# Merge-gate projections as pairs of half-size products ahead of attention, and an attention loop one iteration deeper

## The chip, the core and the metric

The kernel runs on one core of a Trainium2 chip. The metric is the device time of one execution in microseconds, as the median of a few runs; lower is better. The engines are TensorE (PE, matrix products; PEld is its weight load), VectorE (DVE), ScalarE (ACT), GpSimd (POOL) and SyncE (SP, which only issues transfers). Each runs its own instructions in order and waits on semaphores for the others.

## What is computed

One layer of a hybrid trunk on 512 tokens with 1024 channels, all in float32. The parts that matter here:

```python
h = rms_norm(x, mix_norm_pre)
xa, ga, q, k, v, f, g_a, g_b = split(h @ w_in)
y_a = gelu(ga) * rg_lru(causal_dwconv(xa))             # recurrent branch, 1280 channels
y_b = forgetting_attention(q, k, v, f + b_forget)      # 16 heads of 64, per-frame causal
merged = (sigmoid(g_a + b_merge[0]) * (y_a @ w_proj_a)
          + sigmoid(g_b + b_merge[1]) * (y_b @ w_proj_b))
x = x + rms_norm(merged @ w_out, mix_norm_post)
# then: h @ w_up (1024 to 6144), a convolution over 3 tokens, gelu(gate) * value, @ w_down
```

`g_a` and `g_b` are the merge gates: two products of `h` with 1024 x 1024 weights. The sigmoid is computed as a tanh of half the argument; the missing "+1" and "x 0.5" come where the gate is used.

## The kernel before

**Exactness.** PE multiplies in a rounded format, so every float32 operand is split into a high part (a cast on ACT, in lines 172, 696, 756 and others) and a low part (operand minus high part, on DVE, line 175 and others); a product is three matmuls: high x high, high x low, low x high (`mm3`, lines 222 to 224).

**Weights.** `order` lists the weight units in the order in which they are used. `fetch` (through `Split`) loads a unit on SP's queue, casts it and subtracts; `unit(name, ahead)` first fetches up to `ahead` units further. The pool `weights` has four buffers each for raw, high and low tiles, shared by all units.

**Tiles.** A projection tile (`project`) is 128 output channels by 512 tokens: 8 blocks of input channels x 3 matmuls of width 512 into one PSUM bank, of which there are eight.

**Stages.** The recurrent branch's projections (xa, v, ga), then pa, which is `y_a @ w_proj_a` in eight tiles of two units each (order `PA_ORDER`), with transfers for a later stage issued in the background (`background`) and the forget gates (`forget`) within it. Then the attention loop over eight pairs of heads, p = 0 to 7: the q and k tiles; the halves of both; the transposes of the previous pair's probabilities (`pt`); the gate tile ma p, whose tanh multiplies `pa[:, p]` on DVE (line 793); the product with the values for the previous pair (`av`); the scores of this pair (`scores`). `prep_alloc` fills the two bias tiles B (one for each head of a pair; two buffers) on POOL's queue: a broadcast copy from DRAM (line 686), then two adds of the mask by DMA (line 689). `scores` reduces each block of scores with its bias on DVE (line 719), which also frees the bank and, after the last block, the bias tile; the exponentials follow on ACT, and `normalise` scales the rows on DVE. Behind the loop come the mb gate tiles, alternating with pb, which is `y_b @ w_proj_b`, and the merge.

**Pairs.** The up-projection already uses a seven-product scheme (Strassen's, in Winograd's form): two tiles of 128 channels, each 8 blocks by 512 tokens, are seen as 2 x 2 blocks and computed by seven products of half the input channels and half the tokens, 12 matmuls of width 256 each, in place of two tiles of 24 matmuls of width 512. A `Pair` holds two raw weight tiles, splits the plain quarters (`plain_low`, `plain_high`; the low part by a negated cast on ACT and an adding DMA on POOL's queue), forms sums of weight quarters (`sums`, split by `sums_hi` and `sums_lo`) and multiplies with token sums `sh`, `sl`. `keep` copies a partial result that is added to another later. `period` writes out by hand one pair's course, interleaved with the pair before it and the two after it.

**What sets the order.** Most instructions are ordered on each engine by a planner that simulates the program with estimated costs and takes, of what it thinks ready, what was written first. Under `tc.manual_schedule()` (around the up pairs, for example) the written order is kept on every engine. `reuse_waits="tile"` and `bufs` say how many buffers a tile name has: a new tile waits until the last reader of the buffer's former tile has finished, and a pool opened where another was closed waits for the tiles that lay there.

Of the kernel before, what the change touches and what calls it, by code (L numbers as in the profile page):

```python
# [63 lines left out]
def kernel(  # L64
# [124 lines left out]
    order += [(f"pa{e}_{i}", w_pa[2 * e + i], (5, P)) for e, i in PA_ORDER]  # L189
    for p in range(KD):  # L190
        order.append((f"q{p}", *cols(w_in, B_Q + p)))
        order.append((f"k{p}", *cols(w_in, B_K + p)))
        order.append((f"ma{p}", *cols(w_in, B_MA + p)))
    order += [(f"mb{e}", *cols(w_in, B_MB + e)) for e in range(3)]
    for e in range(KD):
        if e >= 3:
            order.append((f"mb{e}", *cols(w_in, B_MB + e)))
        order.append((f"pb{e}", *cols(w_pb, e)))
# [110 lines left out]
    def v_out(c, pv):  # L309
        for t in range(NT):  # L310
            pvv = pv[t].rearrange("p (q j d) -> p q j d", q=4, j=2)
            for q in range(4):
                p = 4 * c + q
                vh = vt[p][:, t, 0:4:3, :]
                act.copy(vh, pvv[:, q])
                dve.tensor_tensor(out=vt[p][:, t, 1:3, :], in0=pvv[:, q], in1=vh.bitcast(F32), op=ALU.subtract)

    with ExitStack() as rg:
# [235 lines left out]
        vpools.append(mstk.enter_context(tc.tile_pool(name="vy1", bufs=5, reuse_waits="tile")))  # L554
        tpool = rg.enter_context(tc.tile_pool(name="rtanh", bufs=TR, side="right", reuse_waits="tile"))
        gpool = rg.enter_context(tc.tile_pool(name="gelu", bufs=2, side="right", reuse_waits="tile"))
# [90 lines left out]

        pps = {}
        for e, half in PA_ORDER:
            if half == 0:  # L650
                pps[e] = bank(f"pa{e}")
            wh, wl = unit(f"pa{e}_{half}")
# [6 lines left out]
            if (e, half) == (4, 1):  # L659
                forget()  # L660

    tgpool = mstk.enter_context(tc.tile_pool(name="tg", bufs=3, reuse_waits="tile"))

    def gate_tile(e, which):
        c = 0 if which == "ma" else KD
        pg = bank(f"{which}{e}")
        project(pg, unit(f"{which}{e}"), hh, hl)
        tg = tgpool.tile([P, S], F32, tag="tg", name=f"tg_{which}{e}")
        act.activation(out=tg, in_=pg, func=AF.Tanh, scale=0.5, bias=hb[:, c + e : c + e + 1])
        return tg  # L670

    with ExitStack() as at:
# [20 lines left out]
        def halves(ps, name):  # L693
            hi = apool.tile([P, S], F32R, tag=f"{name[0]}h", name=f"h_{name}")
            lo = apool.tile([P, S], F32R, tag=f"{name[0]}l", name=f"l_{name}")
            act.copy(hi, ps)
            dve.tensor_tensor(out=lo, in0=ps, in1=hi.bitcast(F32), op=ALU.subtract)
            return hi, lo

        def scores(p, q, k, bias):  # L700
# [11 lines left out]
            for j in range(2):  # L712
                h = 2 * p + j
                Pt = apool.tile([P, PO[NT]], F32, tag="P", name=f"P{h}")
# [46 lines left out]
        def av(p, pts):  # L761
            y = apool.tile([P, S], F32, tag="y", name=f"y{p}", bufs=2)
            tmp = apool.tile([P, S], F32, tag="ytmp", name=f"ytmp{p}", bufs=2)
# [12 lines left out]
            yb[p] = vpools[p == 0 or p > 4].tile([P, 2, S], F32R, tag="vy", name=f"yb{p}")  # L776
            act.copy(yb[p][:, 0], y)
            dve.tensor_tensor(out=yb[p][:, 1], in0=y, in1=yb[p][:, 0].bitcast(F32), op=ALU.subtract)

        prev = None  # L780
        for p in range(KD):
            bias = prep_alloc(p)
            pq, pk = bank(f"q{p}"), bank(f"k{p}")
            project(pq, unit(f"q{p}"), hh, hl)
            if prev is not None:
                normalise(prev)
            project(pk, unit(f"k{p}"), hh, hl)
            q = halves(pq, f"q{p}")
            k = halves(pk, f"k{p}")
            if prev is not None:  # L790
                pts = pt(p - 1, prev)
            tg = gate_tile(p, "ma")
            dve.scalar_tensor_tensor(out=pa[:, p], in0=tg, scalar=1.0, in1=pa[:, p], op0=ALU.add, op1=ALU.mult)
# [17 lines left out]
    ml = mgpool.tile([P, KD, S], F32R, name="ml")  # L811
    for e in range(KD):
        if e >= 3:
            tgs.append(gate_tile(e, "mb"))
        pb = bank(f"pb{e}")
        wh, wl = unit(f"pb{e}")
        for k in range(KD):
            mm3(pb, wh[:, k], wl[:, k], yb[k][:, 0], yb[k][:, 1], k == 0, k == KD - 1)
        tg = tgs[e]
        dve.scalar_tensor_tensor(out=tg, in0=tg, scalar=1.0, in1=pb, op0=ALU.add, op1=ALU.mult)  # L820
# [21 lines left out]
    KH, SH = KD // 2, S // 2  # L842

    def sub(out, a, b):
        dve.tensor_tensor(out=out, in0=a, in1=b, op=ALU.subtract)  # L845

    A, B = slice(0, 512), slice(512, 1024)
    X, Y = slice(0, SH), slice(SH, S)

    def quarter(a, b, s):  # L850
        return tuple(x[:, s].rearrange("p (k e) -> p k e", k=KH) for x in (a, b))

    class Pair:


        def __init__(self, j):
            self.j = j
            self.r = [wpool.tile([P, D], F32, tag="raw", name=f"raw_up{e}") for e in (j, j + JF)]
            for r, e in zip(self.r, (j, j + JF)):
                nc.sync.dma_start(r, w_up[e])  # L860
            self.w, self.t, self.th, self.x, self.ml = {}, {}, {}, {}, {}

        def plain_low(self, i):

            src = self.plain_src(i)
            l = self.ml[i] = stpools[i].tile([P, (D, 512)[i]], F32R, tag=f"ml{i}", name=f"ml{i}_{self.j}")
            act.activation(out=l, in_=src, func=AF.Copy, scale=-1.0)  # L867
            nc.gpsimd.dma_start(l, src, accum_op=ALU.add)  # L868

        def plain_src(self, i):  # L870
            return (self.r[0], self.r[1][:, B])[i]

        def plain_high(self, i):
            src = self.plain_src(i)
            h = stpools[i].tile([P, (D, 512)[i]], F32R, tag=f"mh{i}", name=f"mh{i}_{self.j}")
            act.copy(h, src)
            l = self.ml.get(i)
            if l is None:
                l = stpools[i].tile([P, (D, 512)[i]], F32R, tag=f"ml{i}", name=f"ml{i}_{self.j}")
                sub(l, src, h.bitcast(F32))  # L880
            if i == 0:
                self.w[1], self.w[2] = quarter(h, l, A), quarter(h, l, B)
            else:
                self.w[3] = quarter(h, l, A)

        def plain(self, i):
            self.plain_low(i)
            self.plain_high(i)

        def sums(self, i):  # L890
            r0, r1 = self.r
            t = self.t[i] = tpool.tile([P, D], F32, tag="t", name=f"t{i}_{self.j}")
            if i == 0:
                sub(t[:, A], r1[:, A], r0[:, A])
                sub(t[:, B], r1[:, B], r1[:, A])
            else:
                sub(t[:, A], r1[:, B], self.t[0][:, A])
                sub(t[:, B], r0[:, B], t[:, A])

# [191 lines left out]
    def period(j, n1, n2, load):  # L1091
# [33 lines left out]
        if b:  # L1125
            gelu(b.g)
# [375 lines left out]
```

## Time and profile before

| | us |
|---|---|
| median of 3 runs | 927.29 (927.29 to 927.44) |
| span of the profiled execution, first to last instruction | 924.2 |
| median less that span (the profiled execution's own total isn't printed) | 3.1 |
| granted PE clock over the span | 0.997 |
| pa stage, first matmul of pa to first of q | 190.8 to 248.9 |
| attention loop to the first mb tile | 248.9 to 426.2 |
| mb and pb to the first wo tile | 426.2 to 517.6 |

A profile line of a group reads: line of the kernel, engine, operation, tile written <- tiles read, shape, count, then busy time and mean ns, then the idle time of the engine before it and what ended that. In a timeline line the two first numbers are the start and the length in us. A line number can be that of a helper that many tiles share.

### The profile page before, as it was taken

The page shows a single profiled execution, that of the slowest core. Times are in us where ns is not written, and L with a number is a line of the kernel's source. Part 1 is how long each engine was busy: PE and PEld are TensorE (multiplying, and loading weights), DVE is VectorE, ACT ScalarE, POOL GpSimd, SP SyncE. Part 2 cuts the span into 40 slices and gives each one's busy share as a digit, 9 for nine tenths or more (in the row PEclk, how much of TensorE's full clock was granted, in tenths as well). Part 3 has the DMA queues.
Part 4 walks back from the last instruction along what each step waited for, and adds up shares of the span by engine and source line. Part 5 has one row for each costly group of instructions (what it writes and reads, how often), then busy time and mean ns, then how long its engine had stood idle before and what let it go on. Part 6 is the DMA issues. An engine that isn't in the chain of part 4 may idle for free.

```text
span 924.2 us, 14992 instructions
## 1 busy us (share of the span) xinstructions
PE 911.7 (99%) x5582; PEld 796.1 (86%) x5582; DVE 685.2 (74%) x1121; ACT 568.8 (62%) x982; POOL 230.6 (25%) x240
## 2 busy tenths in 40 slices
PE   8999999999999999999999999999999999999996
PEld 7988888887888888888888889999999999978885
DVE  5866369632857777777644588999999999889897
ACT  7555495433345566666423376688888888676664
POOL 4134345444242232220111000042323323100001
PEclk9999999999999999999999999999999999999998
DMA  7677589989776566553232755188898888799764
GB/s 278 216 227 208 165 207 256 270 211 253 176 229 152 160 148 157 151 150 86 69 114 91 271 182 163 34 212 235 218 238 204 234 208 211 223 372 325 240 201 142
DMA packets 76282, 182.29 MB, mean 197 GB/s; under 512 B 7281, under 2 KB 35745, under 8 KB 75826
## 3 DMA queue, kind: packets, MB, share of 16 engines
q1 hardware_dynamic: 45056, 123.13, 39.5%
q0 software_dynamic: 30864, 57.68, 30.2%
q8 instruction: 44, 0.72, 0.3%
q10 hardware_dynamic: 290, 0.53, 0.1%
q14 instruction: 28, 0.23, 0.1%
HBM read 148.59 MB, written 33.64 MB: 197 GB/s over the span
## 4 chain that ended last, share of the span: by engine, by line
PE 94%; DVE 2%; DMA 1%; issue 1%; ACT 0%; POOL 0%; SPq 0%; DVEq 0%; POOLq 0%
PE up L924 7%; PE up L922 7%; PE up L921 7%; PE dn L1225 4%; PE dn L1224 4%; PE dn L1223 4%; PE pa L223 2%; PE ga L224 2%; PE ga L223 2%; PE pa L224 2%; PE pa L222 2%; PE ga L222 2%; PE q L222 2%; PE ma L222 2%; PE wo L838 2%; PE mb L222 2%
## 5 line engine op out<-in xcount | busy, mean ns | idle before, releaser
L868 POOL DMA_DIRECT2D ml<-raw_up x41 | 35.0, 855 | 154.8 <-ACT ml L867 79.2
L1076 DVE SCALAR_TENSOR_TENSOR u<-up,cpt,u 128x511 f32<-128x511 f32 x96 | 71.2, 745 | 2.6 <-ACT u L1070 0.9
L1225 PE MATMUL dn<-wh_dn,al 128*128 128x512 f32 x168 | 65.6, 391 | 0.9 <-DVE al L845 0.8
L1224 PE MATMUL dn<-wl_dn,ah 128*128 128x512 f32 x168 | 65.4, 389 | 0.0
L1223 PE MATMUL dn<-wh_dn,ah 128*128 128x512 f32 x168 | 65.4, 389 | 0.0
L921 PE MATMUL up<-sh,th 128*128 128x256 f32 x252 | 60.4, 277 | 0.5 <-ACT x L928 0.5
L922 PE MATMUL up<-sl,th 128*128 128x256 f32 x252 | 60.2, 276 | 0.0
L175 DVE TENSOR_TENSOR wl_dn<-raw_dn,wh_dn 128x1024 fp32r<-128x1024 f32 x42 | 51.5, 1226 | 9.1 <-ACT wh_dn L172 9.1
L172 ACT CAST wh_dn<-raw_dn 128x1024 fp32r<-128x1024 f32 x42 | 44.1, 1050 | 17.5 <-issue 10.3
L845 DVE TENSOR_TENSOR tl<-t,th 128x1024 fp32r<-128x1024 f32 x42 | 51.1, 1218 | 1.3 <-ACT th L902 1.3
L1084 POOL TENSOR_TENSOR yf<-u,u 128x512 f32<-128x512 f32 x24 | 32.0, 1333 | 71.8 <-issue 47.5
L1070 ACT ACTIVATE u<-up,cpt 128x512 f32<-128x512 f32 x48 | 36.9, 778 | 19.8 <-PE up L924 11.0
L921 PEld LDWEIGHTS up<-sh,th 128*128 128x128 f32 x252 | 47.3, 188 | 0.7 <-ACT x L928 0.7
L922 PEld LDWEIGHTS up<-sl,th 128*128 128x128 f32 x252 | 47.3, 188 | 0.0
L902 ACT CAST th<-t 128x1024 fp32r<-128x1024 f32 x42 | 43.9, 1045 | 4.5 <-DVE t L845 1.8
L689 POOL DMA_DIRECT2D B<-maskf x32 | 39.1, 1628 | 27.2 <-DMA B<-cnd 24.1
L922 PE MATMUL up<-h2l,mh 128*128 128x256 f32 x168 | 40.2, 276 | 0.0
L921 PE MATMUL up<-h2h,mh 128*128 128x256 f32 x168 | 40.2, 276 | 0.0
L924 PE MATMUL up<-sh,tl 128*128 128x256 f32 x252 | 38.8, 276 | 0.0
L1225 PEld LDWEIGHTS dn<-wh_dn,al 128*128 128x128 f32 x168 | 31.5, 188 | 8.1 <-DVE al L845 1.7
L175 DVE TENSOR_TENSOR wl_pa<-raw_pa,wh_pa 128x640 fp32r<-128x640 f32 x16 | 13.1, 819 | 32.8 <-ACT wh_pa L172 32.8
L1224 PEld LDWEIGHTS dn<-wl_dn,ah 128*128 128x128 f32 x168 | 31.5, 188 | 6.6
(654 smaller groups left out, 3167.7 us busy)
## 6 DMA issues: line engine op xcount, KB each, us to landing
raw_up<-in_w_up_dram SPq DMA_DIRECT2D x48, 512.0 KB, 5.4
td<-in_w_down_dram POOLq DMA_DIRECT2D x36, 512.0 KB, 5.9
raw_dn<-td SPq DMA_DIRECT2D x24, 512.0 KB, 5.0
B<-cnd POOLq DMA_DIRECT2D x16, 640.0 KB, 4.8
ml<-raw_up POOLq DMA_DIRECT2D x20, 512.0 KB, 5.3
raw_dn<-in_w_down_dram SPq DMA_DIRECT2D x18, 512.0 KB, 3.5
raw_wo<-in_w_out_dram SPq DMA_DIRECT2D x16, 512.0 KB, 3.8
td<-td POOLq DMA_DIRECT2D x12, 512.0 KB, 10.8
```

The lines of the kernel that those rows point to most:

```text
L172: act.copy(self.wh, self.raw)
L175: engine.tensor_tensor(out=self.wl, in0=self.raw, in1=self.wh.bitcast(F32), op=ALU.subtract)
L222: pe.matmul(dst, ah, bh, start=first, stop=False)
L845: dve.tensor_tensor(out=out, in0=a, in1=b, op=ALU.subtract)
L902: act.copy(self.th[i], self.t[i])
L921: pe.matmul(dst, wh[:, k], ah[:, k], start=first and k == 0, stop=False, skip_group_check=True)
L922: pe.matmul(dst, wh[:, k], al[:, k], start=False, stop=False, skip_group_check=True)
L924: pe.matmul(dst, wl[:, k], ah[:, k], start=False, stop=k == KH - 1, skip_group_check=True)
L1076: dve.scalar_tensor_tensor(out=c[:, s:], in0=ps[:, : S - s], scalar=col(C_CFW + 3 * e + j), in1=c[:, s:], op0=ALU.mult, op1=ALU.add)
L1223: pe.matmul(dst[t], ah[:, k, tok], wh[:, k], start=first, stop=False, skip_group_check=True)
L1224: pe.matmul(dst[t], ah[:, k, tok], wl[:, k], start=False, stop=False, skip_group_check=True)
L1225: pe.matmul(dst[t], al[:, k, tok], wh[:, k], start=False, stop=last, skip_group_check=True)
```

## The change

- Fourteen of the sixteen merge-gate tiles (ma 0 to 7, mb 0 to 5) become seven pairs of the seven-product scheme, in a stage of their own between pa and attention. `Pair` and `period` move up and take their source block, token sums, pools and epilogue as parameters (`Halved`). The up-projection uses the same classes as before.
- The token sums of `h` and the first gate pair's weight sums are formed within the pa stage (`early_sums`, called after each of its 16 steps); `forget` moves from the step (4, 1), the tenth, to the fourth.
- The tile mb6 is computed alone between pa and the first pair; the tile mb7 alone in the last attention iteration.
- An ma gate multiplies `pa` at once; an mb gate is written to DRAM (`gmb`) and read back while pb runs.
- After the last pair come q0 and k0, whose weights are fetched within the hand-written order.
- The attention loop has no gate tile. In iteration p: scores of p, the q tile of p + 1, transposes of p - 1, the k tile of p + 1 and both halves, av of p - 1, normalise of p. The probabilities get four buffers in place of two; the halves of q and k and one small tile get one in place of two.
- Parts of pb 0, 1 and 2 are computed at the end of attention; the rest behind it.

The core of the diff:

```diff
+            elif step == 12:
+                gp[0] = Pair(gates, 0, GP[0])
+            elif step == 13:
+                gp[0].sums(0)
+                gp[0].sums(1)
...
-            wh, wl = unit(f"pa{e}_{half}")
+            wh, wl = unit(f"pa{e}_{half}", min(2, len(PA_ORDER) - step))
...
+    def gate_use(name, tg):
+        e = int(name[2])
+        if name[:2] == "ma":
+            dve.scalar_tensor_tensor(out=pa[:, e], in0=tg, scalar=1.0, in1=pa[:, e], op0=ALU.add, op1=ALU.mult)
+        else:
+            nc.sync.dma_start(gmb[e], tg)
...
+    gate_tile("mb6", 0)
+    with ExitStack() as g2:
...
+        gp[1] = Pair(gates, 1, GP[1])
+        man = g2.enter_context(ExitStack())
+        man.enter_context(tc.manual_schedule())
+        for i, f in enumerate((fq[3], fq[0], fq[2], fq[1])):
+            act.copy(gates.sh[i], f)
+            sub(gates.sl[i], f, gates.sh[i].bitcast(F32))
...
+        p.plain_high(0)
+        p.plain_high(1)
+        p.p5()
+        p.p12()
+        n.sums(0)
+        n.sums(1)
+        n.plain_low(0)
+        p.keep(2, p.a[:, Y])
+        p.add(p.a[:, X], p.a[:, X], 2)
+        p.keep(1, p.c[:, X])
...
+        def more(j):
+            if j + 3 < len(GP):
+                gp[j + 3] = Pair(gates, j + 3, GP[j + 3])
+            elif j + 2 < len(GP):
+                pass
+            else:
+                fetch(where[("q0", "k0")[j + 2 - len(GP)]])
+
+        for j in range(len(GP)):
+            period(gp[j], gp.get(j - 1), gp.get(j + 1, none), gp.get(j + 2, none), gate_epilogue, lambda: more(j))
+            gp.pop(j - 1, None)
+        b = gp.pop(len(GP) - 1)
+        b.add(b.c[:, Y], b.a[:, Y], 1)
+        b.add(b.c[:, X], b.c[:, X], 0)
+        gate_epilogue(b, "c", 0)
+        pq = bank("q0")
+        project(pq, unit("q0", 0), hh, hl)
+        gate_epilogue(b, "c", 1)
+        pk = bank("k0")
+        project(pk, unit("k0", 0), hh, hl)
+        b.product(4, b.a[:, Y])
...
         for p in range(KD):
-            bias = prep_alloc(p)
-            pq, pk = bank(f"q{p}"), bank(f"k{p}")
-            project(pq, unit(f"q{p}"), hh, hl)
-            if prev is not None:
-                normalise(prev)
-            project(pk, unit(f"k{p}"), hh, hl)
-            q = halves(pq, f"q{p}")
-            k = halves(pk, f"k{p}")
+            now = scores(p, q, k, bias)
+            if p < KD - 1:
+                bias = prep_alloc(p + 1)
+                pq = bank(f"q{p + 1}")
+                project(pq, unit(f"q{p + 1}"), hh, hl)
+            else:
+                gate_tile("mb7", 2)
             if prev is not None:
                 pts = pt(p - 1, prev)
-            tg = gate_tile(p, "ma")
-            dve.scalar_tensor_tensor(out=pa[:, p], in0=tg, scalar=1.0, in1=pa[:, p], op0=ALU.add, op1=ALU.mult)
+            if p < KD - 1:
+                pk = bank(f"k{p + 1}")
+                project(pk, unit(f"k{p + 1}"), hh, hl)
+                q, k = halves(pq, f"q{p + 1}"), halves(pk, f"k{p + 1}")
+            else:
+                pb_part(0, range(KD - 2))
             if prev is not None:
                 av(p - 1, pts)
-            prev = scores(p, q, k, bias)
-        tgs = [gate_tile(0, "mb")]
-        normalise(prev)
-        tgs.append(gate_tile(1, "mb"))
+            normalise(now)
+            prev = now
         pts = pt(KD - 1, prev)
-        tgs.append(gate_tile(2, "mb"))
+        pb_part(1, range(KD - 1))
         av(KD - 1, pts)
+        pb_part(0, range(KD - 2, KD - 1))
+        pb_part(2, range(KD - 1))
```

More of the change, by code (lines that the diff above doesn't have):

```diff
@@ L189 @@
     order += [(f"pa{e}_{i}", w_pa[2 * e + i], (5, P)) for e, i in PA_ORDER]
+    order.append(("mb6", *cols(w_in, B_MB + 6)))
     for p in range(KD):
@@ L192 @@
         order.append((f"k{p}", *cols(w_in, B_K + p)))
[L193 to L198, printed above, removed]
+    order.append(("mb7", *cols(w_in, B_MB + 7)))
+    order += [(f"pb{e}", *cols(w_pb, e)) for e in range(KD)]
     for ph in range(2):
@@ L658 @@
                 act.copy(pa[:, e], pps[e])
[L659 to L669, printed above, removed]
-        return tg
+            early_sums(step)
@@ L672 @@
+    dstk.close()
     with ExitStack() as at:
```

405 lines of the change are left out of this document (254 added, 151 removed).

## The prediction

> **What bounds the kernel now.** I read the page, then the waits of TensorE (PE), the matmuls of single tiles, the chain of waits, the table of stages, and last the timelines of one attention iteration.
>
> ```profile
> span 924.2 us, 14992 instructions
> PE 911.7 (99%) x5582; PEld 796.1 (86%) x5582; DVE 685.2 (74%) x1121; ACT 568.8 (62%) x982; POOL 230.6 (25%) x240
> PE 94%; DVE 2%; DMA 1%; issue 1%; ACT 0%; POOL 0%; SPq 0%; DVEq 0%; POOLq 0%
> ```
>
> PE is busy for 99% of the span and carries 94% of the chain that ended last. The waits of PE (line, releaser, us in total, times, longest) hold only a few us; two of them matter here:
>
> ```profile
> PE up L924 <- DMA ml<-raw_up: 0.9, 1, 0.9
> ...
> PE up L921 <- ACT x L928: 0.5, 1, 0.5
> ```
>
> So the time falls by what PE no longer executes, unless a new wait appears. These two, 1.4 us together, stand where the up-projection begins its half-size products; the change builds a second such beginning.
>
> How long is a tile, and how long a pair? Busy times overlap (matmuls are pipelined), so I take distances between starts. The ga tiles' row gives first and last start (us) of the first matmul of each group of three; the chain gives the same place of the pair loop ten pairs apart.
>
> ```profile
> L222 PE MATMUL ga<-hh,wh_ga x80: 389/389/390, 136.4 to 190.1; 128*128 128x512 f32 x80
> ```
> ```profile
> 621.33 0.45 PE up L924 x4
> ...
> 716.93 0.45 PE up L924 x4
> ```
> ```profile
> 621.33:716.93 95.60, 95.60 (x842) 95.60 (x842) 89.45 (x133) 79.62 (x121) 30.28 (x31) 1.00 0.89 224
> 190.80:249.00 58.20, 58.20 (x258) 47.10 (x257) 27.96 (x35) 19.80 (x29) 23.63 (x27) 1.00 0.97 214
> 301.25:323.94 22.69, 22.69 (x154) 19.06 (x156) 16.65 (x43) 13.82 (x34) 4.95 (x7) 1.00 0.58 156
> 437.40:517.60 80.20, 80.20 (x394) 66.84 (x394) 39.11 (x39) 27.56 (x40) 8.98 (x7) 1.00 0.32 102
> ```
>
> From 136.4 to 190.1 lie 79 groups of three matmuls: 0.2266 us each, 5.44 us for a tile of 24. Ten pairs of seven products run in 95.60 us: 9.56 us a pair of 84 half-width matmuls, 0.114 us each, 1.37 us a product. In the table (length; busy PE, weight load, DVE, ACT, POOL; clock; DMA share; GB/s) PE is full in all four stages and the clock is 1.00.
>
> **The change, term by term.**
>
> *The products.* A gate pair has the same 84 matmuls, of the same shapes and alternation, as an up pair. Fourteen tiles cost 14 x 5.44 = 76.2 us, seven pairs 7 x 9.56 = 66.9: **9.2 us less** PE work. In that stage the other engines do less than in the up stage, where DVE was busy 89.45 of 95.60 with the convolution taps and PE waited for nothing; the gate stage has two tanh and at most two DVE products a pair instead of four taps. So the steady gate periods are put at 9.56 with no wait. The Trainium skill, "TensorE: Matmul & The Clock Gate" (Back-to-back issue gap), speaks for a smaller gain: it gives N/2.4 + 2.5 ns, a fixed part for each matmul that seven half-size products pay 84 times and two tiles 48 times; by that a pair would save an estimated 1.2 us, the seven 8.3. The trace has 0.114 against 0.227, a ratio of one half with no fixed part left to see, and it decides.
>
> *Work put before the gates.* Beside the pa products DVE gets eight 1024-wide adds or subtractions for the token sums, four 512-wide ones for the first pair and two 1024-wide splits; ACT two casts. Their lengths, and those of what leaves the attention loop (four iterations, mean ns after the bar):
>
> ```profile
> L175 DVE TENSOR_TENSOR wl_ma<-raw_ma,wh_ma 128x1024 fp32r<-128x1024 f32 x4 | 4.9, 1224 | 13.9 <-ACT wh_ma L172 13.9
> L793 DVE SCALAR_TENSOR_TENSOR pa<-tg_ma,pa 128x512 f32<-128x512 f32 x4 | 2.7, 684 | 0.0
> ```
> ```profile
> L172 ACT CAST wh_ma<-raw_ma 128x1024 fp32r<-128x1024 f32 x5 | 5.2, 1047 | 19.5 <-issue 19.5
> L669 ACT ACTIVATE tg_ma<-ma,hb 128x512 f32<-128x512 f32 x4 | 2.7, 680 | 0.0
> ```
>
> 10 x 1.22 + 4 x 0.68 = 14.9 us of DVE go into a stage with 30 us free: nothing, unless one blocks a weight split in DVE's order. The first pair's 1 MB comes over DMA engines that are 97% busy there; its raw tiles are needed some 10 us later, and I count nothing.
>
> *The beginning of the gate stage.* PE's cover is the mb6 tile, 5.44, and p5, 1.37. Meanwhile ACT casts four token sums (4.2 us) and DVE subtracts them (4.9), then splits the plain quarter. If they start with mb6, they fit. If ACT's order puts the tanh of mb6 first, p5 waits 0.68 + 1.05 + 1.22 = 2.95, and the low part of product 1, due at 2.95 + 1.37 + 0.91 = 5.23, waits for five DVE subtractions, 0.68 + 1.05 + 6.1 = 7.8: 5.5 in all. Between 0 and 5.5 I take the 1.4 that the other such beginning shows: **+1.4**.
>
> *q0 and k0 fetched in the hand-written order.* Their cast and split stand in ACT's and DVE's order ahead of the sums of the next pair. The cast of q0 needs one of four buffers, and two pairs hold all four until product 7. Then 1.05 + 1.22, and two adds of this kind:
>
> ```profile
> 638.62 0.43 DVE L940 TENSOR_TENSOR up<-up,x 128x256 f32<-128x256 f32 x1
> ```
>
> together 3.1, against two products, 2.73, that PE has meanwhile: **+0.4**, from 0 to 2 if the load lands late behind the gate writes on SP's queue. Behind k0's split stand only adds that 10.9 us of q0 and k0 cover.
>
> *Attention.* One iteration of PE before (start, us):
>
> ```profile
> 301.18 0.71 PE L746 MATMUL pt<-ident,P 64*128 64x64 f32 x16
> ...
> 302.56 0.50 PE L222 MATMUL ma<-hh,wh_ma 128*128 128x512 f32 x1
> ...
> 308.14 0.39 PE L770 MATMUL av<-PTh,v 128*128 128x512 f32 x1
> ...
> 310.71 0.49 PE L710 MATMUL s4c<-h_k,h_q 64*128 64x512 f32 x1
> ...
> 312.78 0.50 PE L222 MATMUL q<-hh,wh_q 128*128 128x512 f32 x1
> ...
> 318.34 0.39 PE L222 MATMUL k<-hh,wh_k 128*128 128x512 f32 x1
> ```
>
> Transposes 1.4, ma 5.6, av 2.6, scores 2.1, q 5.6, k 5.5. Without ma the loop is 22.7 - 5.6 = 17.1 us. DVE keeps 16.65 - 1.22 - 0.68 = 14.75 of it, ACT 12.1: busier, not the bound. Two covers shrink. First, k's halves: before, the transposes and ma lay between k and av; now only av does.
>
> ```profile
> 303.32 0.68 DVE L697 TENSOR_TENSOR l_k<-k,h_k 128x512 fp32r<-128x512 f32 x1
> ...
> 306.71 0.47 DVE L757 TENSOR_TENSOR PTl<-pt_r,PTh 128x128 fp32r<-128x128 f32 x2
> ```
>
> l_k ended at 304.0, 2.8 us after k (301.18), with a weight split just ahead of it; the second matmul of scores needs it 2.6 + 0.3 after k. That is even: **+0.7** (0.1 in each of seven), from 0 to 3.5. Second, the bias tiles B. There are two, for the even and the odd head, refilled only after the reductions of scores have read them, by a copy and two masked adds each, in order on POOL's queue:
>
> ```profile
> 312.99 0.68 DVE L719 CUSTOM_DVE_ANT_0 P<-s5c,B 128x512 f32<-128x512 f32 x1
> ...
> 316.27 0.08 DVE L719 DVE_READ_ACCUMULATOR2_ANT mx<- 128x1 f32 x1
> ```
> ```profile
> 315.96 1.25 POOL L686 DMA_DIRECT2D B<-cnd  x2 [13.42 <-DVE mx L719]
> 320.98 2.46 POOL L689 DMA_DIRECT2D B<-maskf  x2 [3.76 <-DMA B<-cnd]
> 323.89 2.40 POOL L689 DMA_DIRECT2D B<-maskf  x2 [0.45 <-DMA B<-cnd]
> ```
> ```profile
> DMA to landing us min/median/max: 3.0/5.5/7.6
> ```
>
> (The last line is that of all masked adds.) The odd tile is first read at 313.0 and free at 316.35; its last add is issued at 325.1 and lands at a median 5.5 later, 330.6. The loop of this buffer is 17.6 us: hidden in 22.7, even with 17.1. The transposes need the score banks 2.1 + 5.6 = 7.7 after scores begin, the reductions end 5.6 after (316.35): 2 us of slack. The first iteration has neither transposes nor av, so the second scores follow after 2.1 + 5.6 + 5.5 = 13.2, 4.4 before the odd tile: 4.4 - 2 = **+2.4**, once. It is 0 if DVE takes the reductions in another order, 6 if the first B must also wait for gate tiles in the same memory, which are read until q0.
>
> *The end.* The transposes' copies took from 301.18 to 307.2, 6.0; in the last iteration 18 matmuls of pb0 (4.1) and the transposes (1.4) cover them: **+0.5**, 0 to 1.5. The mb gates go through DRAM, 2 MB out and 2 MB back, the latter in a stage with a DMA share of 0.32: nothing.
>
> **Sum:** -9.2 + 1.4 + 0.4 + 0.7 + 2.4 + 0.5 = **-3.8 us** on a span of 924.2. The runs' median, 927.29, has 3.1 us around the span, which nothing here touches: **923.5**. By the bounds it is from -9.2 (918.1) to +9.3 (936.6).
>
> **Rivals.** *Every cover holds* (-6.5 to -9.2, about 919): for it, the up stage has run this sequence without a wait and the loop's engines have 14% or more left; against it, three margins are even. Chance 0.22. *The bias loop becomes the bound, and the kernel gets slower*: one landing at 7.6 in place of 5.5 makes the loop 19.7, 2.6 more than PE's 17.1, and what is late stays late: seven iterations lose 18, less 2 of slack, 16, in place of the 2.4 above, +10 in all (937). It decides from a loop of 18.5, where 7 x 1.4 - 2 = 7.8 with the other 3.0 eats the 9.2 and more. For it: refills closer together raise the DMA share; against it: landings at the median. With 1.6 a loop over PE's in place of 2.6 it is 930. Chance 0.19. *The gain comes and is given back* at several of these places, within 0.2%: 0.12. The rest, 0.47, is the forecast, -1.9 to -6.5; in it lies that half-size products keep a fixed cost which the up stage doesn't show (the 0.9 less gain of the page's rule, 924.4), a chance of 0.02 after the ratio above.
>
> Faster by over 0.2% (1.9 us, about what a measurement here can tell from no change) is 0.47 + 0.22 = 0.69; slower 0.19. The range, 918.6 to 930.0, leaves out the very best and the upper half of the slow case.
>
> **What would show it.** Right: seven gate periods of 9.56, an attention loop of 17.1 to 17.6, and PE waits of 3 to 8 us in all, for the gate sums at the start, for DVE's reductions at the first transposes, and for l_k. The bias rival: POOL's adds landing after scores in every iteration, a loop over 18.5. Wrong altogether: gate periods over 9.56, or waits in pa for weight splits behind the token sums.

## The result: slower by 0.9%, and the profile after

| | before | after |
|---|---|---|
| median, us (range, runs) | 927.37 (927.29 to 928.62, 4) | 936.65 (934.84 to 937.35, 4) |
| span of the profiled execution | 924.2 | 935.6 |
| end of pa to first wo matmul | 248.9 to 517.6 | 249.0 to 526.8 |

The ratio of the times is 1.0091, 95% interval 1.0076 to 1.0105; by the medians the change costs 9.3 us, where 3.8 less were forecast. The profiled execution of the kernel after is the slowest of its four, 937.35 us. The page of the kernel after says so in three lines: its span, TensorE's busy time, and the shares of the chain that ended last.

```profile
span 935.6 us, 15714 instructions
PE 911.4 (97%) x5834; PEld 803.7 (86%) x5834; DVE 724.7 (77%) x1184; ACT 596.9 (64%) x1033; POOL 243.1 (26%) x252
PE 84%; DMA 7%; DVE 3%; issue 3%; POOL 1%; ACT 1%; SPq 0%; DVEq 0%; POOLq 0%; ACTq 0%
```

PE carried 94% of the chain before and carries 84% now; transfers have 7%. The table of stages finds the place (length; busy PE, weight load, DVE, ACT, POOL; clock; DMA share; GB/s). The stages are the gate pairs, q0 to product 4, attention's opening from S(0) to the end of S(2), one steady iteration, and mb7's start to the first wo. S(p), PT(p), av(p) are scores, transposes and the product with the values of iteration p.

```profile
254.44:326.06 71.62, 68.12 (x578) 67.31 (x576) 46.93 (x68) 47.35 (x73) 11.42 (x15) 1.00 0.67 176
326.06:338.56 12.50, 12.49 (x64) 10.41 (x62) 5.37 (x7) 5.80 (x8) 3.05 (x3) 1.00 0.93 296
338.56:382.33 43.77, 36.95 (x225) 28.76 (x225) 26.95 (x74) 20.76 (x53) 14.53 (x14) 0.92 0.74 190
382.33:399.73 17.40, 17.40 (x131) 14.58 (x129) 14.84 (x42) 12.18 (x32) 6.02 (x6) 1.00 0.68 168
469.31:526.79 57.48, 57.47 (x330) 48.04 (x329) 39.01 (x71) 26.49 (x56) 13.39 (x7) 1.00 0.43 148
```

Two stages have holes: the gate pairs (3.5 us) and the opening of attention (6.8 us of 43.77, and the only clock below 1.00). The steady iteration is full. PE's waits between 245 and 385 us name them:

```profile
PE s2c L981 <- ACT h_k L967: 4.5, 1, 4.5
PE ma L409 <- DMA gml<-raw_ma: 1.7, 1, 1.7
PE ma L406 <- DVE ma L425: 1.3, 1, 1.3
PE s4c L981 <- DVE l_k L968: 1.0, 1, 1.0
PE s0c L981 <- DVE l_k L968: 0.6, 1, 0.6
```

S(1) waits 4.5 us for h_k, a cast of 0.58 us. Why is it late? The chain of waits, PE's pieces left out (start, length):

```profile
324.71 3.70 DMA raw_k<-in_w_in_dram
...
328.43 1.06 ACT wh_k L172
...
329.51 0.22 DVE wl_k L175
...
330.65 0.44 DVE mb L425
...
331.64 0.57 POOL B L957
...
332.49 0.75 POOL B L960
333.25 13.31 DMA B<-maskf
...
352.13 4.13 DMA B<-cnd
...
359.60 7.60 DMA B<-maskf
```

POOL's timeline shows the link in the middle, ACT's the last one:

```profile
316.99 0.55 POOL L957 DMA_DIRECT2D B<-cnd  x1 [2.68 <-DVE gtl L318]
...
331.64 0.57 POOL L957 DMA_DIRECT2D B<-cnd  x1 [13.78 <-DVE mb L425]
332.49 2.48 POOL L960 DMA_DIRECT2D B<-maskf  x2 [0.28 <-issue]
341.62 2.39 POOL L960 DMA_DIRECT2D B<-maskf  x2 [6.66 <-DMA B<-cnd]
```
```profile
347.47 0.72 ACT L995 ACTIVATE P<-P,mx 128x512 f32<-128x512 f32 x1 [7.43 <-DVE mx L990]
...
350.49 0.72 ACT L995 ACTIVATE P<-P,mx 128x512 f32<-128x512 f32 x1 [2.20 <-DVE mx L990]
...
356.52 0.58 ACT L967 CAST h_k<-k 128x512 fp32r<-128x512 f32 x1
```

Read them in order. A load of raw_k is issued late, behind the last gate writes on SP's queue; ACT's cast and DVE's split of it come late, and DVE's addition for the last gate pair (L425) stands behind that split. The odd bias tile lies over the x1 tile that this addition reads, so its copy stands 13.8 us on POOL, with the *even* tile's masks, whose own copy had long been issued, queued behind it. The first of those masks lands after 13.3 us, among the loads of q and k (DMA share 0.93). The maxima start at 346.7 instead of behind S(0), at 341.5; the exps wait for them; h_q(1) and h_k(1) stand behind the exps on ACT. Then S(1) is 4.5 us late, the next bias copies, which wait for the maxima, go out at 352.1, and the whole repeats once, weaker.

In the kernel before, nothing held the odd copy: it went out 1.9 us behind the even one, and the first maxima followed at 268.1.

```profile
254.90 0.58 POOL L686 DMA_DIRECT2D B<-cnd  x1 [17.00 <-DMA cnd<-f_cum]
...
256.75 0.58 POOL L686 DMA_DIRECT2D B<-cnd  x1
```

### The profile page after: what moved, and what is told of

It is laid out like the page before. It is cut to its first block, busy times and chain, and to the rows that moved or that the text cites. A ratio compares the mean times of both kernels' runs of the same rounds, so it can differ in the third digit from the quotient of the medians.

```text
span 935.6 us, 15714 instructions
## 1 busy us (share of the span) xinstructions
PE 911.4 (97%) x5834; PEld 803.7 (86%) x5834; DVE 724.7 (77%) x1184; ACT 596.9 (64%) x1033; POOL 243.1 (26%) x252
## 4 chain that ended last, share of the span: by engine, by line
PE 84%; DMA 7%; DVE 3%; issue 3%; POOL 1%; ACT 1%; SPq 0%; DVEq 0%; POOLq 0%; ACTq 0%
PE up L406 6%; PE up L409 6%; PE up L407 6%; PE dn L1390 4%; PE dn L1388 4%; PE dn L1389 4%; DMA B<-maskf 2%; PE ga L221 2%; PE ga L220 2%; PE ga L219 2%; PE pa L220 2%; PE pa L219 2%; PE pa L221 2%; PE pb L219 2%; PE wo L1129 2%
## 5 line engine op out<-in xcount | busy, mean ns | idle before, releaser
L995 ACT ACTIVATE P<-P,mx 128x384 f32<-128x384 f32 (+2 forms) x64 | 35.2, 552 | 20.7 <-DVE mx L990 19.8
L353 ACT ACTIVATE ml<-raw_up 128x512 fp32r<-128x512 f32 (+1 forms) x41 | 34.2, 833 | 6.6 <-DMA raw_up<-in_w_up_dram 6.6
```

## The experiments

Each kernel was timed beside runs of the kernel before on the same chip (medians 927.34 to 927.84). The changed kernel itself was not run again on those chips, so the ratios are what to compare.

| run | edit | median, us | ratio to before, 95% |
|---|---|---|---|
| (after) | | 936.65 | 1.0091, 1.0076 to 1.0105 |
| e1 | bias tiles first in memory | 938.10 | 1.0105, 1.0080 to 1.0130 |
| e2 | gate rows written from ACT | 932.72 | 1.0058, 1.0037 to 1.0079 |
| e3 | e1 + e2 | 936.03 | 1.0089, 1.0074 to 1.0104 |
| e4 | first low part on DVE | 935.36 | 1.0075, 1.0051 to 1.0099 |
| e5 | bias over memory free by 318 us | 930.67 | 1.0029, 1.0013 to 1.0045 |
| e6 | h_q, h_k ahead of the first exps | 933.16 | 1.0060, 1.0041 to 1.0078 |
| e7 | 10 matmuls added ahead of k1 | 936.38 | 1.0095, 1.0072 to 1.0119 |
| e8 | e4 + e5 + e6 | 929.74 | 1.0015, 1.0003 to 1.0028 |
| e9 | e8 + e2 + token sums first | 928.69 | 1.0009, 0.9997 to 1.0021 |
| e10 | e9 + 6 matmuls added | 928.51 | 1.0012, 1.0001 to 1.0022 |
| e11 | 19 matmuls added ahead of S(1) | 936.50 | 1.0098, 1.0083 to 1.0113 |
| e12 | gates as whole tiles | 932.70 | 1.0059, 1.0039 to 1.0079 |
| e13 | e9 + mb7 in iteration 0 | 928.32 | 1.0007, 0.9996 to 1.0018 |
| e14 | e13 + first addition first | 930.90 | 1.0041, 1.0024 to 1.0057 |
| e15 | after + mb7 in iteration 0 | 937.88 | 1.0117, 1.0104 to 1.0130 |
| e16 | e2 + e4 + e5 + e14's two | 929.33 | 1.0028, 1.0015 to 1.0041 |
| e17 | e13 + pb parts placed anew | 926.70 | 0.9994, 0.9985 to 1.0003 |
| e18 | e2 + e4 + e5 + mb7 and pb as in e17 | 925.94 | 0.9996, 0.9986 to 1.0007 |

**e1: the bias tiles out of x1's memory.**

```diff
+        bpool = at.enter_context(tc.tile_pool(name="bias", bufs=2, reuse_waits="tile"))
         apool = at.enter_context(tc.tile_pool(name="attn", bufs=2, reuse_waits="tile"))
...
-                B = apool.tile([P, PO[NT]], F32, tag="B", name=f"B{h}")
+                B = bpool.tile([P, PO[NT]], F32, tag="B", name=f"B{h}")
```

> The edit moves only the memory of the bias tiles: they get a pool of their own, opened ahead of the other attention tiles, so that the second one no longer lies over the x1 tile that the last pair's addition on VectorE still reads. Theory 1 (the opening: the odd bias copy waited 13.8 us on POOL's queue behind that addition, the even tile's mask adds stood behind it, the late maxima held the exps and with them h_k on ScalarE): the wait of 4.5 us for h_k goes, reductions of iteration 0 start near 341 instead of 346.7 us, PT(0) takes its usual 1.4 us, and the time falls by 5 to 8 us, to 929-932. Theory 2 (late q and k loads, behind the gate writes on SP's queue and in a burst, are what delays the opening): no more than 2 us is gained, 934.5-936.5, and the wait for h_k stays at 3 us or more.

No gain. The mask tile, now first in the pool `attn`, took the place over x1, and POOL's whole queue waited:

```profile
332.73 0.21 POOL L948 MEMSET maskf<- 128x128 f32 x1 [20.95 <-DVE mb L425]
...
342.83 4.90 POOL L961 DMA_DIRECT2D B<-maskf  x4 [8.24 <-DMA B<-cnd]
```

S(1) waited 4.8 us. The edit moved POOL's wait and did not remove it, so this run decides nothing between the theories.

**e2, e3: the gate writes off SP's queue.**

```diff
-            nc.sync.dma_start(gmb[e], tg)
+            act.dma_start(gmb[e], tg)
```

> The edit issues the seven writes of gate rows for tiles mb0 to mb6 and mb7 from ScalarE's queue, behind the tanh that makes them, instead of from SP's; the loads of q and k behind them on SP no longer wait for a tanh. Theory 1 (odd bias copy behind the last pair's addition): the loads come 1 to 3 us earlier, the bias tiles as late as before; the gain is under 2 us, 934.5-936.7. Theory 2 (loads of q0, k0, q1, k1 held on SP and in a burst with the masks): raw_k lands some 4 us earlier, the masks of the first bias tile no longer take 13 us, and the time falls by 3 to 6 us, 931-934.

> Both edits together. Theory 1: as the first alone, 929-932, the second adding under 1 us. Theory 2: as the second alone, 931-934. If both are links of one chain, the gain is more than the sum of the two alone.

e2 gains 0.33%, and S(1)'s wait for h_k falls from 4.5 to 1.4 us: the second theory's number. The odd copy still waited for the same addition, which came 3.3 us sooner (328.3 instead of 331.6). The first mask still took 11.3 us. This speaks for two links of one chain, SP's queue its beginning and x1's memory its middle. The gain above the sum that e3 should have shown didn't come: the memory of e1 undoes the gain.

**e4: the first low part.**

```diff
         n.sums(1)
-        n.plain_low(0)
         p.keep(2, p.a[:, Y])
```

> Pair 1's first low part is made by a subtraction on VectorE instead of by an adding DMA (issued on POOL's queue at 258.1 us, landed after 8.6 us, TensorE waiting 2.0 us for it). Theory of the gate stage's start (the wait is the DMA's latency): TensorE's waits at the start fall from 4.8 to about 3 us, the time by 1.5 to 2 us, 934.6-935.2. Rival (VectorE is the bound of the start, since its additions ahead of products 6 and 3 already come 1.3 us late): the new subtraction of 1024 elements delays the others, and the time stays within 0.7 us of 936.65 or gets up to 1.5 us longer.

The wait of 1.7 us is gone from the trace; the median fell by 1.3 us, but the intervals overlap. It agrees with the latency theory and doesn't prove it.

The profiled execution of e4 is the fastest of its six (929.66 us; they reach 937.75) and shows something else. The odd copy waited 13.7 us on POOL as before, but the first mask landed after 9.2 us instead of 13.3, S(1) waited 1.6 us for h_k and 1.0 for l_k, and the clock stayed at 1.00. So the late copy alone doesn't fix the loss: the landing of the mask behind it adds to it, and small differences between single profiles prove little.

**e5: the same theory as e1, done properly.** `bias` holds the mask as well, and two early memsets turn x2 and x1 by one buffer.

```diff
+                for i in (2, 1):
+                    pad = gates.kpool.tile([P, SH], F32, tag=f"x{i}", name=f"gx{i}_pad", bufs=2)
+                    pool.memset(pad, 0.0)
...
+        bpool = at.enter_context(tc.tile_pool(name="bias", bufs=2, reuse_waits="tile"))
...
-        maskf = apool.tile([P, P], F32, name="maskf", bufs=1)
+        maskf = bpool.tile([P, P], F32, name="maskf", bufs=1)
```

> The first of these runs moved the second bias tile off the x1 tile, but put the mask tile onto it, and POOL's whole queue then waited for the same addition (until 332.7 us). This one moves both: bias tiles and mask in a pool of their own opened first, and the gates' x1 and x2 tiles turned by one buffer (two small memsets early in the pa stage), so that everything the bias needs lies over memory whose last reader is done by about 318 us. Theory 1 (POOL's wait at the opening): both copies are issued at 317-319 and land by 328, all masks are in by about 338, the maxima of iteration 0 follow S(0) at about 341, and h_k(1) is there when k1 ends; TensorE's wait for it falls from 4.5 us to under 1.5, the clock stays granted, and the time falls by 5 to 9 us, to 928-932. Rival (burst of loads on the DMA engines): copies and masks are issued early but land just as late, and less than 3 us is gained.

```profile
321.16 0.57 POOL L961 DMA_DIRECT2D B<-cnd  x1 [4.19 <-DVE mb L425]
...
326.79 2.39 POOL L964 DMA_DIRECT2D B<-maskf  x2 [2.29 <-DMA B<-cnd]
```
```profile
PE s2c L985 <- ACT h_k L971: 1.4, 1, 1.4
```

The copies are out by 321.7 us, the masks by 329 instead of 344, S(1) waits 1.4 us, PT(0) takes 1.4 us instead of 2.9, and the ratio falls by 0.62%, 5.8 us. Nothing but where tiles lie was changed, the two memsets aside. This is the cause of most of the loss, as shown. One sign was missed: the clock did not stay up (last section).

**e6: the other end of the chain.** `run_exps` holds the loop of exps, called for iteration 0 behind the halves.

```diff
+                with tc.issue_after(kcopy[0].ins):
+                    run_exps(late)
```

> In iteration 0 ScalarE's eight exps are placed behind the copies h_q(1) and h_k(1) (and VectorE's maxima of iteration 1 behind the normalising of iteration 0); nothing else changes, the bias tiles come as late as before. If the order on ScalarE is what holds S(1): h_k(1) is done some 0.6 us after k1 ends, S(1) waits for VectorE's release of the banks at most (1 us instead of 4.5), and the exps, 4 us later, delay PT(0) by 0 to 2 us; the time falls by 3 to 6 us, 930.5-933.5. If the late bias is what counts, wherever the wait is taken, the exps come late for PT(0) and the whole is given back there: within 1.5 us of 936.65.

3 us gained and S(1)'s wait for h_k down to 1.4 us, with the bias as late as ever: ACT's order is a link too.

**e7, e11, e10: is it the clock?** In the opening the granted clock fell to one half (windows of 3 us; the last three columns are clock, DMA share, GB/s):

```profile
354.00:357.00 3.00, 0.00 (x0) 0.00 (x0) 2.96 (x10) 3.00 (x6) 0.45 (x1) 0.63 0.97 352
357.00:360.00 3.00, 2.76 (x10) 1.62 (x12) 2.66 (x4) 0.10 (x1) 3.00 (x4) 0.50 0.59 98
360.00:363.00 3.00, 3.00 (x22) 2.60 (x21) 0.00 (x0) 0.00 (x0) 1.47 (x2) 0.73 1.14 237
```

Matmuls whose result is overwritten were put where PE idles: in e7 ten ahead of k1, in e11 nineteen and in e10 (on the mended kernel) six between k1 and S(1).

```diff
+            if p == 1:
+                for i in range(19):
+                    pe.matmul(regs[0][3], wk1[0][:, i % KD], hh[:, i % KD], start=i == 0, stop=i == 18)
```

> Ten matmuls of 512 columns (10 x 0.2266 = 2.3 us of TensorE work whose result is overwritten) are put ahead of projection k1, into the time in which TensorE waits for h_k. Clock theory (in the profiled run the granted clock fell to 0.50 from about 355 to 362 us, some 2.5 us after TensorE had run dry, and S(1), q2 and PT(0) ran at half speed): the idle time is cut to 2.2 us, the clock stays at 1.00, and the time falls by 1.5 to 3.5 us although work was added: 933-935. Rival (the half speed has another cause, or the delays behind S(1) are waits for other engines): the idle time is filled and nothing follows, 936.0-937.3; if h_k moves with the end of k1, 2.3 us are lost, 939.

> The changed kernel itself with 19 matmuls of 512 columns (4.3 us, result overwritten) between projection k1 and S(1), where TensorE waits 4.5 us for h_k. No wait of another engine is touched. Clock theory: no half speed at 355-362 us, S(1) takes 2.1-2.4 us and q2 5.3-5.7 instead of 10.2 together; the time falls by 1.5 to 3 us, to 933.6-935.1, although 4.3 us of work was added. Rival (what follows S(1) waits for the late bias tiles of iteration 1, and the half speed hides under that): the mask adds of iteration 1 still land at about 364, PT(0) and S(2) take up what S(1) gained, and the time is within 0.7 us of 936.65.

> The same with six matmuls of 512 columns (6 x 0.2266 = 1.4 us, result overwritten) between projection k1 and S(1), where TensorE waits 1.4 us for h_k. Clock theory (half speed for 3.4 us or twice that follows a stretch with idle time at the opening): the granted clock stays at 1.00 in 350-370 us, and the time is 1 to 2 us below that of the kernel without them. Rival: the half speed comes all the same, or S(1) starts late; equal or up to 1 us longer.

e7 left 2.2 us idle and the clock fell all the same. In e11 it stayed up:

```profile
357.00:360.00 3.00, 1.44 (x12) 0.86 (x12) 3.00 (x4) 1.05 (x1) 2.37 (x4) 1.00 0.62 171
```

And the time is that of the changed kernel. So the half speed goes with the idle time in front of it: it came with 2.2 us left idle (e7) and not with 1.6 (e11), one profile each. But it cost nothing that can be measured here: the masks of iteration 1 are issued at 357.6 (356.6 without the filling), and PT(0) and S(2) wait for what hangs on them. My clock theory falls; the rival written beside it holds. e10's clock was up with and without its six matmuls, so that run tests nothing of it.

**e12: no pairs.** The fourteen gates as whole tiles in the same place. The token sums, the pair tiles in memory and the hand-written order go with the pairs.

```diff
+    gate_tile("mb6", 2)
+    for w, n in (("ma", 8), ("mb", 6)):
+        for e in range(n):
+            gate_tile(f"{w}{e}", 2)
```

> The fourteen gate tiles computed as whole tiles at the place of the pairs (14 x 5.44 = 76.2 us), with the rest of the change kept: attention without ma tiles and one iteration deeper, gate rows stored. No token sums, no pair tiles in memory. The pairs' stage took 71.6 us and its last product 1.6, so TensorE has 3.0 us more to do. If the opening's loss came from memory shared with the pairs' tiles, it goes too: S(1) waits under 1.5 us, 6 to 8 us are gained there, and the time is 931-934, below that of the changed kernel although no product is saved. If the opening's loss belongs to the deeper attention itself, the time is 938.5-940.5.

4 us faster than the pairs although PE has 3.0 us more to do. Without pair tiles in memory the first bias goes out ahead of the gates, at 243.9 and 244.9 us, and S(0) and S(1) wait 1.4 us each, for h_k: that is what a scores stage waits when nothing stands between k and it.

```profile
244.90 0.68 POOL L884 DMA_DIRECT2D B<-cnd  x1
```

**e8, e9: the mended kernel.** e9 adds e2 and places the token sums ahead of pair 0's sums with `issue_after`.

> Bias free early, halves ahead of the exps, and pair 1's first low part on VectorE. If the opening's waits are one chain that any of the two former removes, the sum is that of the bias edit and about 2 us from the gate stage's start: 926-930, the steady loop unchanged at 17.4 us a period. If the start's gain is given back, 928-932.

> The edits of the run before (bias free early, halves ahead of the exps, first low part on VectorE), and two more: the token sums hf go ahead of pair 0's weight sums on VectorE (which waited 4.3 us for raw_ma at 231.6 us with the token sums queued behind), and the gate rows are written from ScalarE's queue (TensorE waited 0.9 us in k0 for a raw_k that stood behind such a write on SP). If the start of the gate stage is VectorE's lateness: its waits of 2.5 us there fall under 1 us, k0 takes 5.44 us, and the time falls by 2 to 3.5 us from 929.7, to 926.2-927.7: at or just below the kernel before. If the start waits for something else (raw loads of pair 1), under 1 us is gained, 929-930.

From e5 to e8 to e9 the ratio falls a little each time, within the intervals; by the medians 8 us of the 9.3 are regained and the kernel before is not beaten. For e9 I had expected 926.2 to 927.7. In both, the start of the gates keeps its waits of 1.2 and 1.3 us: the order of the token sums was not their cause.

**e15, e13: more cover.** Cover is work of PE placed where it would otherwise wait for another engine. mb7 moved from iteration 7 to iteration 0, between k1 and S(1).

```diff
-                gate_tile("mb7", 2)
...
+                if p == 0:
+                    gate_tile("mb7", 2)
```

> The changed kernel with that one move alone: mb7 from iteration 7 to iteration 0, between k1 and S(1). The bias tiles stay as late as they were (odd copy behind the last pair's addition, masks behind it). If the loss at the opening is that nothing of TensorE's covers the late maxima, S(1)'s wait of 4.5 us for h_k goes, the clock stays up, PT(0) comes in time, and 5 to 8 us are gained: 929-932. If every later bias tile runs late by the same amount (its copy waits for the maxima of the iteration before), the wait moves to PT(0) and S(2), and 1.5 to 4 us are gained: 933-935.

> The mended kernel (bias free early, halves ahead of the exps, first low part on VectorE, token sums first, gate rows written from ScalarE) with the whole gate tile mb7 (24 matmuls, 5.44 us) moved from iteration 7, where the normalised scores of the last pair are ready 7.1 us before they are used, to iteration 0 between projection k1 and S(1), where TensorE waits 1.4 us for h_k and 1.0 us for l_k in S(2). If those waits are a lack of cover, both go, nothing appears at the end, and the time falls by 2.0 to 2.6 us, from 928.7 to 926.1-926.7: below the kernel before. If the end then waits for the last pair, half or more is given back, 927.5-928.7.

```profile
PE pt_r L1018 <- DVE mx L991: 4.3, 2, 3.9
```

On the changed kernel (e15) S(1)'s wait for h_k goes, and PT transposes wait 4.3 us for the maxima instead, with the clock at one half behind it: 5.4 us of cover doesn't buy back a late bias, and I expected too much. On the mended kernel (e13) the waits at S(1) and S(2) go, but at the end PT(6), which needs the score banks of S(7), waits for VectorE:

```profile
PE pt_r L1036 <- DVE mx L1001: 2.3, 1, 2.3
```

I had read the slack of the last pair's scaled scores (7 us) and not that of the banks.

**e14, e16: the first addition ahead of pair 1's sums.** The edit of e14 against e13:

```diff
-        n.sums(0)
-        n.sums(1)
         p.keep(2, p.a[:, Y])
         p.add(p.a[:, X], p.a[:, X], 2)
         p.keep(1, p.c[:, X])
+        n.sums(0)
+        n.sums(1)
```

> The same, and at the start of the gate stage pair 0's first addition on VectorE is placed ahead of pair 1's sums (2.8 us), behind which it was 1.3 us late for product 6. If that order is the cause, TensorE's wait of 1.3 us there goes and the time is 1.0 to 1.5 us below the run without it: 924.8-925.6. If pair 1's sums then come late for its own products, the wait moves by one period and the gain is under 0.4 us.

> Bias free early, gate rows from ScalarE, mb7 as cover in iteration 0, first low part on VectorE and pair 0's addition first, but ScalarE's exps of iteration 0 in their old place and the token sums in theirs. If the reordering of the exps only mended what the cover mends too, the time is that of e14 within 0.8 us; if it is still needed, h_k(1) or PT(0) waits and the time is 1 to 3 us longer.

Slower by 0.34%: PE's waits there became 0.9 us for the addition and 2.7, in two pieces, for ACT's gmh, where e13 has 1.3 and 1.2. The gate pairs up to q0 take 72.6 us in e14 and 72.3 in e16, which has the same edit, against 70.6 in e13. So the order of that one addition alone was not what held the start; the waits moved along the queues of DVE and ACT. The profile of e14 is the slowest of twelve (937.71 us) and has a wait of 4.8 us at the end as well, so not all of its loss need come from the start. e16 came out 1.6 us below e14, with overlapping intervals, where I had expected the same time or more.

**e17, e18: a cover at the end.** Six of eight parts of pb0 before PT(6), six of pb1 before av(6), the rest behind PT(7).

```diff
+            if p == KD - 1:
+                pb_part(0, range(KD - 2))
             if prev is not None:
                 pts = pt(p - 1, prev)
```

> The mended kernel with mb7 in iteration 0, and the parts of the pb projections at the end placed anew: six of eight parts of pb0 between S(7) and PT(6) (4.1 us, where TensorE waited 2.3 us for VectorE to release the banks), six of pb1 between PT(6) and av(6), then the seventh parts of both and four of pb2 between PT(7) and av(7). No work is added or taken away. If that wait was what the move of mb7 cost, the end has no wait and the time is 1.5 to 2.5 us below the 928.3 of the version with the move alone: 925.8-926.8, below the kernel before by 0.1 to 0.2%. If the gain is lost elsewhere (weights of pb, banks), 928-929.

> The same end, with ScalarE's exps of iteration 0 and the token sums in the places that the changed kernel gave them, and pair 0's addition behind pair 1's sums as there. If cover and memory are all that the opening lacked, the time is within 0.7 us of the run beside it; if the late exps matter, h_k(1) or PT(0) waits and it is 1 to 2 us above.

e17's wait for the banks is gone and 1.6 us with it, as expected, and like e18 it ties with the kernel before. e18 shows that the reordered exps and token sums aren't needed beside the other edits (e2, e4, the memory and the cover): ACT's order may stay as the changed kernel has it. Neither kernel is faster than before by more than the interval.

## Why the prediction was wrong

From the end of pa to the first wo matmul the profiled executions took 268.7 us before and 277.8 after, 9.1 more. By the prediction's own terms:

| term | predicted (bounds) | profile after | from |
|---|---|---|---|
| products | -9.2 | -7.7 | 7 x 9.78 - 76.2 |
| start of the gate stage | +1.4 (0 to 5.5) | +4.7 | 71.62 + product 4, 1.61, - 68.5 |
| q0 and k0 | +0.4 (0 to 2) | 0 | no wait of PE |
| cover of k's halves | +0.7 (0 to 3.5) | +3.0 | S(0) 0.6, S(1) 1.4 as in e5, S(2) 1.0 |
| first bias tiles | +2.4 (0 to 6) | +8.1 | 43.77 - 32.7 - 3.0 |
| end | +0.5 (0 to 1.5) | 0 | no wait of PE |
| steady loop | 17.1 | 17.40, 5 loops: +1.5 | table of stages |
| sum | -3.8 | +9.6 | 9.1 by the two ends |

(32.7 is the opening without waits: a loop of 17.4, and S(0), q1, k1 and S(1) by the lengths before.) The profiled spans differ by 11.4; the rest lies outside this stretch. The medians differ by 9.3.

- **The step that failed most is the first bias tile: +2.4 was taken, +8.1 came.** The prediction named its mechanism ("6 if the first B must also wait for gate tiles in the same memory, which are read until q0"), and then took 2.4. It also let those reads end at q0 (326.1), while the addition that reads x1 ended at 331.1, behind the split for k0. That memory is reused can be worked out from the pools' order and sizes; I treated it as a case, not as something to look up. The bound of 6 was too small as well: I priced the buffer and its transfers, and left out that POOL's queue holds the even tile's masks behind the odd tile's copy, that a mask can take 13.3 us among a burst of loads when the longest seen before was 7.6, and that ACT's order puts h_k behind the exps. For the mb gates through DRAM the forecast put "nothing", by bandwidth; their place on SP's queue it priced only at q0 and k0, up to 2, where PE did not wait. The cost came behind them, at the opening (e2).
- **It was not the only one.** The terms miss by 13.4 us in all, 5.7 of them here. With 2.4 in its place the other terms would still give +3.9: product speed, the start, k's halves and the loop eat the gain by themselves. e5, which mends the memory alone, is still slower than the kernel before (1.0029).
- **The slower rival had the right sign and the wrong mechanism.** Its bias loop of more than 18.5 us did not come: from iteration 3 the loop is 17.40, PE full. The bias was late at the opening, through memory, and its time of 930 to 937 fits by accident. So does the sum of the forecast's upper bounds, +9.3: two of its terms came to nothing and one went past its bound.
- **The start of the gates** lay within its bounds, near the upper end. The reason is the one feared, DVE's and ACT's queue there, and one not listed: product 1's low part of pair 1 waited 1.7 us for an adding DMA of 8.6 us.
- **The products** came out 0.22 us a pair dearer than in the up stage. Periods start at 268.78, 278.55 and 288.33, and the matmuls with sums of weights (gth) take 5 ns more than those with plain weights (gmh); the up stage has 277 ns for the first kind:

```profile
278.55 0.28 PE L406 MATMUL ma<-gsh,gth 128*128 128x256 f32 x1
...
288.33 0.28 PE L406 MATMUL ma<-gsh,gth 128*128 128x256 f32 x1
```
```profile
L406 PE MATMUL ma<-gsh,gth 128*128 128x256 f32 x41 | 10.2, 281 | 0.0
...
L407 PE MATMUL mb<-hl,gmh 128*128 128x256 f32 x24 | 5.7, 276 | 0.0
```
```profile
L406 PE MATMUL up<-sh,th 128*128 128x256 f32 x212 | 51.0, 277 | 1.6 <-DVE up L425 1.1 <-ACT x L413 0.5
```

Its cause was not tried and stays open. It was "wrong altogether: gate periods over 9.56" in the prediction's list, and is 1.5 of the 13.4 us.
- **k's halves** were the right kind of wait in the wrong place: not 0.1 in each of seven iterations, but 3.0 in S(0), S(1) and S(2), and nothing stands between k1 and S(1). **The steady loop** has no wait of PE at 17.40; its scores take 2.20 us instead of 2.07 and q 5.65 instead of 5.56, and why was not tried.

What the mended kernels show is the size of what was there to win: e18's profile takes 267.1 us (249.6 to 516.8) where the kernel before took 268.7, and its ratio of 0.9996 is a tie. Of the 9.2 us of products, 1.5 for slower matmuls, some 3 at the start of the gates and 1.5 for the longer loop remain lost there; no edit here won them back.

## What to carry to other kernels

When a change opens a stage in memory that another stage just left, list, for every tile of the new stage that a transfer fills, the last reader of what lay there, and what else stands in the issuing queue behind it: e5 changed nothing else and gave back 5.8 us. A wait is only removed if nothing took its place: look at the same queue again (e1), and at every engine that a cover was serving before it is moved (e13: it also gave VectorE time to release banks). And a busy share that has a hole in one stage of 44 us tells more than the page's 97%.

## What the runs showed of the hardware that was not expected

The clock came down in two lengths. A window whose mean clock is 0.63 spent 0.74 of its time at 0.50. So in the changed kernel the three windows above give 0.74 + 1.00 + 0.54 of 3 us at half speed, 6.8 us; in e5 it was half of that:

```profile
354.00:357.00 3.00, 2.85 (x18) 2.11 (x20) 1.96 (x3) 0.10 (x1) 0.00 (x0) 0.81 1.26 192
357.00:360.00 3.00, 3.00 (x18) 2.56 (x15) 2.90 (x16) 2.74 (x9) 0.49 (x1) 0.62 0.23 94
```

0.38 + 0.76 of 3 us, 3.4. The Trainium skill, "TensorE: Matmul & The Clock Gate" (Part 1, What's actually happening), has a free-running window of 3.4 us after which the clock is halved or restored: the lengths agree, one window and two. It gives a whole idle window as the condition; here e5 had only 1.4 us of idle time at one stretch before it, so less than a whole idle window was enough. e9, with the same 1.4, had no fall at all, nor had e4 with 1.6 and 1.0; what decides between them no run shows. e11 shows that such a fall need not cost anything when another chain sets the end.

The masks of a bias tile are 128 KB each (count, size, median us to landing, 310 to 420 us):

```profile
B<-maskf POOLq DMA_DIRECT2D x20, 128.0 KB, 6.1
```

The Trainium skill, "DMA: Bandwidth & Descriptors" (Anatomy of one DMA, SWDGE path), fits 2.0 us plus the bytes over 436e3 per us, an estimated 2.3 us. The trace has 6.1 at the median and 13.3 for the one that mattered, issued among loads of q and k (DMA share 0.93 in that stage); the measurement decides. That the loads are the reason for the 13.3 was not tried alone, and the same mask took 9.2 in e4.
